# A two-layer mixture of experts that streams its weights from HBM: longer contiguous runs per partition, and fewer groups of 128 slots

## The chip, the cores and the metric

The kernel runs on one core of one Trainium2 chip. The metric is the device time of one execution in microseconds. The time before is 2375.89 us, the median of 3 runs (2375.29 to 2379.04).

## The reference, cut to what matters

The model is a block with two layers (attention, a mixer, then a mixture of experts) followed by a second block with two more layers and no experts. Only the mixture of experts is touched. It has 32 experts in 4 groups of 8; each token goes to 2 experts, and layer 0 has 512 tokens (`x` and `ctx`), layer 1 has 256.

```python
def run(args):                      # one block of token rows, one expert e
    xb, e = args
    return (jax.nn.silu(xb @ w1[e]) * (xb @ w3[e])) @ w2[e]
...
ys = lax.map(run, (xs, block_e)).reshape(-1, d_)
return jnp.zeros_like(h).at[slot_tok].add(ys * slot_gate[:, None])
```

`w1[e]` and `w3[e]` are 1024x512 float32, `w2[e]` is 512x1024 float32: 2 MB each, 6 MB an expert, 192 MB a layer, and all of it is read from HBM in each layer.

## The kernel before, in words

**Weights.** All large weights go through one stream of units of 1 MB (class `Stream`, tiles `wu`, 128 partitions x 2048 float32), issued in a fixed order by SP. A unit takes a free slot; SP waits at the DMA until the matmuls that last read the slot are done. In the experts' stage there are 10 slots in layer 0 and 11 in layer 1 that go round, and 3 more that are used once (`SLOTS`, `EXTRA`). An expert's weights are pushed by `push_ex` (L203): its number is in a register, and the unit holds `per` chunks of 128 rows of the matrix, 4 for `w1` and `w3`, 2 for `w2`. So an expert is 6 units: two for each matrix. Chunk `k` of the unit is row block `k`: partition `p` gets row `k*128 + p`, so that a partition's 8 KB come as 4 runs of 2 KB (`w1`, `w3`) or 2 runs of 4 KB (`w2`).

**Slots and groups.** The experts are ranked by their number of tokens (expert 0 always stands first, its units are loaded before the routing is known). `CAPS` (L43) gives rank by rank how many token slots an expert gets: 128 (or 256), 64 or 32. A group is 128 slots: one expert of 128 (kind `b`), two of 64 (`m`) or four of 32 (`s`). `make_plan` (L49) makes the groups; `ORDER` (L45) puts them into blocks. Before there are 16 groups in layer 0 (6 `b`, 7 `m`, 3 `s`) and 15 in layer 1 (7 `b`, 3 `m`, 5 `s`, the second expert having two `b` groups that share their weights). Where an expert has more tokens than its slots, a flag is set and a slow branch (`fallback`, L1347) runs over all experts.

**Work of a block** (`moe_main`, L1158). For each group stage A multiplies by `w1`, stage B by `w3`, stage C by `w2`; in a block all A come first, then all B, then all C. The four (two) experts of a group work in different columns of the PE array, so that a stage of a group has the same number of steps whatever its kind. A half stage needs the units of its half of *all* the group's experts, and hands them back at its end.

- *Gather* (`prep`, `step`, L1184): the block's token rows are brought into slots and transposed by matmuls of a one-hot matrix `G` with the tokens, kept as a pair of float32r tiles (`tok0h`, `tok0l`, in the second layer `tok1h`, `tok1l`). The tokens are the stationary operand, 128 columns `k*128 .. k*128+127` for chunk `k`; a chunk takes 2 matmuls per 128 tokens, 8 in layer 0 and 4 in layer 1. The next block's four steps stand in this block's C stages.
- *Transposes* (`tr`, L1311): before stage C the 128x512 product `sil` is transposed in four pieces.
- *Scatter* (`scatter`, L1222): a group's result goes back to the token rows by 16 matmuls in layer 0 (8 in layer 1), DVE multiplies by the gate row and POOL adds.

All matmuls are recorded at line 276, all transposes at line 314, the experts' DMAs at line 207.

Of the kernel before, what the change touches and what calls it, by code (L numbers as in the profile page):

```python
# [14 lines left out]
def _warn_once_fixed(msg, *args, **kwargs):  # L15
# [16 lines left out]
P = 128  # L32
# [7 lines left out]
NE = 32  # L40

NSTATIC = 1
CAPS = {4: [128] * 6 + [64] * 14 + [32] * 12,  # L43
        2: [128, 256] + [128] * 4 + [64] * 6 + [32] * 20}
ORDER = {4: ("bs", "bmmb", "smbm", "mbsm", "bm"),  # L45
         2: ("bs", "bbsm", "sbm", "sbm", "bsb")}


def make_plan(caps, order):  # L49


    lists = {"b": [], "m": [], "s": []}
    p = 0
    while p < len(caps):
        c = caps[p]
        if c >= P:
            lists["b"] += [(P, [p], b) for b in range(0, c, P)]
            p += 1
        else:
            n = P // c  # L60
            assert caps[p:p + n] == [c] * n
            lists["m" if c == 64 else "s"].append((c, list(range(p, p + n)), 0))
            p += n
    groups, blocks, stages = [], [], []
    for i, pat in enumerate(order):
        ids = list(range(len(groups), len(groups) + len(pat)))
        groups += [lists[ch].pop(0) for ch in pat]
        blocks.append(ids)
        seq = [(z, g) for z in "ABC" for g in ids]
        if i == 0:  # L70
            a, b = ids
            seq = [("A", a), ("B", a), ("A", b), ("B", b), ("C", a), ("C", b)]
        stages += [(i, z, g) for z, g in seq]
    assert not any(lists.values())
    return groups, blocks, stages


def constants():
# [16 lines left out]
    col = np.stack([31 - i + np.where(i < NSTATIC, 1 << 20, 0), i], 1).astype(f)  # L95
    cap4 = np.tile(np.array(CAPS[4], f), (P, 1))
    cap2 = np.tile(np.array(CAPS[2], f), (P, 1))
    out["cst_a"] = np.concatenate([ident, sel2, iota, rcol, w4, w8, col, cap4, cap2], 1)
# [40 lines left out]
class Stream:  # L139
# [62 lines left out]

    def push_ex(self, src, reg, k0, per, n):  # L203

        def fn(t):
            r = reg()
            self.last = self.nc.sync.dma_start(  # L207
                t[:, :per * n].rearrange("p (k f) -> p k f", k=per),
                src[ds(r, 1), k0 * P:(k0 + per) * P, :].rearrange("o (k p) f -> p (o k) f", p=P)).ins
        self.push(fn, 2)  # L210

    def get_kn(self, ks, n):
# [20 lines left out]
class Kern:  # L233
# [859 lines left out]
    def static_experts(self, l, NT):  # L1093
        if l:
            for c in range(0, D, 256):
                self.ws.push_kn(self.a["w_mk_2"][0][:, c:c + 256], KD, 256, 1, self.tc.issue_after(self.bc_last))
        groups, blocks, stages = self.plans[NT] = make_plan(CAPS[NT], ORDER[NT])
        n = 0
# [59 lines left out]
    def moe_main(self, l, NT, pl, tok, acc, G2, mp0, end_plan, load_numbers):  # L1158
# [4 lines left out]
        with ExitStack() as es:  # L1163
# [5 lines left out]
            def prep(b):  # L1169

                gb = [groups[g] for g in blocks[b]]
                n = len(gb) * P
                G = T([P, NT, 512], "G", 1, F32R)
                for i, (w, ps_, base) in enumerate(gb):
                    nj, p0 = len(ps_), ps_[0]
                    nc.vector.tensor_tensor(
                        G[:, :, i * P:(i + 1) * P].rearrange("p t (j w) -> p t j w", j=nj),
                        self.iota[:, base:base + w][:, None, None, :].to_broadcast([P, NT, nj, w]),
                        pl["pos"][:, :, p0:p0 + nj][:, :, :, None].to_broadcast([P, NT, nj, w]),
                        op=OP.is_equal)  # L1180
                Gf = G.bitcast(F32)
                xq = []

                def step(q):  # L1184
                    xt = T([P, 2, 512], "xT", 4)
                    for kk in range(2):
                        k = 2 * q + kk
                        ps = self.pt("t")
                        for t in range(NT):
                            for z, src in enumerate((tok.hi, tok.lo)):  # L1190
                                self.mm(ps[:, :n], src[:, t, k * P:(k + 1) * P], G[:, t, :n],
                                        t == 0 and z == 0, t == NT - 1 and z == 1)
                        self.ev(xt[:, kk, :n], ps[:, :n])
                    xq.append(xt)

                def gates():
                    pgate = self.pt("s")
                    for i, (w, ps_, base) in enumerate(gb):
                        for t in range(NT):
                            for j, p in enumerate(ps_):  # L1200
                                self.mm(pgate[w * j:w * (j + 1), i:i + 1],
                                        Gf[:, t, i * P + w * j:i * P + w * (j + 1)], pl["gs"][:, t, p:p + 1],
                                        t == 0, t == NT - 1)
                    gcol = T([P, 4], "gcol", 2)
                    nc.vector.tensor_copy(gcol[:, :len(gb)], pgate[:, :len(gb)])
                    return gcol
                return dict(xq=xq, step=step, gates=gates)

            def rows(g):
# [53 lines left out]
            for si, (b, z, g) in enumerate(stages):  # L1263
# [9 lines left out]
                if z in "AB":  # L1273
                    ps = self.pt("mm")
# [33 lines left out]
                h_ = sil.pop(g)  # L1308
                tp = self.pt("t")
                for f in range(4):  # L1310
                    self.tr(tp[:, f * P:(f + 1) * P], h_[:, f * P:(f + 1) * P])  # L1311
                hT = T([P, 4, P], "hT", 2)
                self.ev(hT.rearrange("p f s -> p (f s)"), tp)
                if not any(zz == "B" and bb == b for bb, zz, _ in stages[si:]) and b + 1 < len(blocks):
# [852 lines left out]
```

## Time and profile before

| | before |
|---|---|
| median of 3 runs | 2375.89 us |
| the profiled execution, its own time | 2375.62 us |
| its span, first to last instruction | 2374.0 us |
| experts of layer 0 on PE (A, B, C and all between) | 351 to 885 us of the span |
| experts of layer 1 on PE | 1120 to 1640 us of the span |
| moved by all DMAs | 598.60 MB, of it 384 units of the experts |
| PE busy | 2170.5 us (91%) |

A page of the profile shows one execution: busy time per engine, 40 slices of the span with the busy share of each engine, of the 16 DMA engines and their GB/s, the chain that ended last, and groups of like instructions. PE's busy time counts from an instruction's start to its end, with overlaps merged; matmuls follow each other faster than one of them lasts. A DMA share above 1 is possible, since packets of one DMA engine overlap.

### The profile page before, as it was taken

To read this page: it belongs to the slowest core of one execution; us is meant where nothing else is said; L and a number is where in the kernel's file an instruction comes from. 1 tells how busy PE (TensorE), PEld (TensorE's weight loads), DVE (VectorE), ACT (ScalarE), POOL (GpSimd) and SP (SyncE) were. 2 spreads that over 40 slices of the span, in tenths; PEclk is the share of its full clock that TensorE was granted. 3 is DMA by queue.
4 is the path that set the end of the run, shared out by engine and by line. 5 is a ranking of instruction groups with operands and counts; after the bars stand their busy time and mean duration, and the time that the engine had idled before them with its cause. 6 is when DMAs were issued, how large, how long until landed. Compare 5 with 4: busy or idle time off the path is not lost.

```text
span 2374.0 us, 32289 instructions
## 1 busy us (share of the span) xinstructions
PE 2170.5 (91%) x12723; PEld 1390.7 (59%) x12723; DVE 1004.6 (42%) x1963; ACT 702.8 (30%) x1267; POOL 399.9 (17%) x377
## 2 busy tenths in 40 slices
PE   7999979999998998998888887979999899999898
PEld 4565454443443436656333232325989799998797
DVE  3562562223131447624202212214566665565664
ACT  3344110010010114431110000002568464557653
POOL 0000221214051543012101202112100200100211
PEclk9998969999999998999889888989999899999999
DMA  9444569999999986464999999998444244443341
GB/s 311 137 132 167 200 215 345 387 351 334 400 391 385 401 319 220 156 216 170 342 337 384 384 400 387 400 386 293 152 143 138 91 164 142 143 155 113 107 142 46
DMA packets 330764, 598.60 MB, mean 252 GB/s; under 512 B 22218, under 2 KB 132330, under 8 KB 330604
## 3 DMA queue, kind: packets, MB, share of 16 engines
q1 hardware_dynamic: 322782, 579.22, 67.7%
q0 software_dynamic: 3728, 13.17, 1.6%
q10 hardware_dynamic: 4094, 4.05, 0.5%
q8 instruction: 103, 1.69, 0.3%
q14 instruction: 57, 0.47, 0.1%
HBM read 595.30 MB, written 1.10 MB: 251 GB/s over the span
## 4 chain that ended last, share of the span: by engine, by line
PE 36%; DMA 9%; issue 4%; DVE 2%; ACT 1%; SPq 1%; POOL 0%; DVEq 0%; ACTq 0%; POOLq 0%
PE psmm L276 31%; DMA wu<-in_w_dram 8%; PE pss L276 4%; PE pst L276 1%; PE pst L314 1%; SPq L207 1%; ACT wsplit L289 1%; DVE wsplit L293 1%; DVE yg L1231 0%; DMA c<-in_cst_dram 0%; DVE xd L1881 0%; DVE cvy L1863 0%; POOL mixA1l L293 0%; ACT dM L1922 0%; ACT yh L1339 0%
## 5 line engine op out<-in xcount | busy, mean ns | idle before, releaser
L276 PE MATMUL psmm<-wu,xT 128*32 128x512 f32 (+2 forms) x2080 | 480.4, 654 | 82.6 <-DMA wu<-in_w_dram 72.7
L276 PEld LDWEIGHTS psmm<-wu,xT 128*32 128x32 f32 (+2 forms) x2080 | 157.4, 144 | 370.0 <-issue 277.3
L1233 POOL TENSOR_TENSOR xs<-xs,yg 128x512 f32<-128x512 f32 x120 | 151.9, 1282 | 700.2 <-DVE yg L1231 699.6
L276 PE MATMUL psmm<-h2Th,wsplit 128*128 128x256 f32 x1344 | 258.1, 288 | 4.7 <-ACT zg L1850 3.7
L276 PE MATMUL psmm<-wu,hT 128*32 128x512 f32 (+2 forms) x1040 | 233.9, 633 | 17.0 <-DMA wu<-in_w_dram 16.9
L293 DVE TENSOR_TENSOR wsplit<-wu,wsplit 128x2048 fp32r<-128x2048 f32 x86 | 198.6, 2311 | 60.9 <-ACT wsplit L289 60.1
L276 PEld LDWEIGHTS psmm<-h2Th,wsplit 128*128 128x128 f32 x1344 | 212.9, 191 | 8.4 <-ACT zg L1850 3.9
L1231 DVE TENSOR_TENSOR yg<-pss,G 128x512 f32<-128x512 f32 x176 | 116.8, 687 | 231.5 <-PE pss L276 224.3
L289 ACT CAST wsplit<-wu 128x2048 fp32r<-128x2048 f32 x86 | 163.6, 1902 | 109.5 <-PE psmm L276 77.0
L276 PE MATMUL psmm<-h2Tl,wsplit 128*128 128x256 f32 x672 | 192.5, 287 | 0.0
L276 PEld LDWEIGHTS psmm<-wu,hT 128*32 128x32 f32 (+2 forms) x1040 | 76.4, 139 | 145.6 <-issue 123.5
L1289 DVE TENSOR_TENSOR sil<-sil,psmm 128x512 f32<-128x512 f32 x31 | 21.3, 687 | 317.6 <-PE psmm L276 317.6
L1339 ACT ACTIVATE yh<-psmm,gcol 128x512 fp32r<-128x512 f32 x62 | 41.8, 687 | 295.8 <-PE psmm L276 172.1
L276 PEld LDWEIGHTS psmm<-h2Tl,wsplit 128*128 128x128 f32 x672 | 128.5, 191 | 1.1 <-issue 0.7
L1287 ACT ACTIVATE sil<-psmm 128x512 f32<-128x512 f32 x31 | 18.5, 598 | 275.6 <-PE psmm L276 275.6
L276 PE MATMUL pss<-yh,S 128*128 128x512 f32 x176 | 86.1, 489 | 11.2 <-DVE yg L1231 9.9
L259 ACT COPY xT<-pst 128x512 f32<-128x512 f32 (+2 forms) x36 | 17.8, 497 | 247.7 <-PE psmm L276 146.1
L276 PE MATMUL psmm<-wu,mixT 128*128 128x512 f32 x192 | 90.4, 623 | 0.0
L1341 DVE SCALAR_TENSOR_TENSOR yl<-psmm,gcol,yh 128x512 fp32r<-128x512 f32 x62 | 45.9, 747 | 94.3 <-ACT yh L1339 93.2
L1233 POOL TENSOR_TENSOR cs<-cs,yg 128x512 f32<-128x512 f32 x62 | 77.9, 1278 | 46.1 <-DVE yg L1231 46.1
L519 DVE TENSOR_REDUCE mx<-psmm 128x1 f32<-128x256 f32 (+2 forms) x128 | 53.5, 452 | 50.0 <-PE psmm L276 49.8
L276 PEld LDWEIGHTS pss<-yh,S 128*128 128x128 f32 x176 | 33.1, 188 | 66.7 <-issue 33.5
(582 smaller groups left out, 3966.8 us busy)
## 6 DMA issues: line engine op xcount, KB each, us to landing
wu<-in_w_dram SPq DMA_DIRECT2D x384, 1024.0 KB
wu<-in_w_in_dram SPq DMA_DIRECT2D x62, 1024.0 KB
wu<-in_w_ada_dram SPq DMA_DIRECT2D x48, 1024.0 KB
wu<-in_w_out_dram SPq DMA_DIRECT2D x24, 1024.0 KB
wu<-in_w_mv_dram SPq DMA_DIRECT2D x8, 1024.0 KB
wu<-in_w_mq_dram SPq DMA_DIRECT2D x8, 1024.0 KB
wu<-in_w_mo_dram SPq DMA_DIRECT2D x8, 1024.0 KB
wu<-in_w_mk_dram POOLq DMA_DIRECT2D x4, 1024.0 KB, 12.1
```

The source lines that it names most:

```text
L207: self.last = self.nc.sync.dma_start(t[:, :per * n].rearrange("p (k f) -> p k f", k=per), src[ds(r, 1), k0 * P:(k0 + per) * P, :].rearrang ...
L276: return self.nc.tensor.matmul(out, lhsT, rhs, start=start, stop=stop).ins
L289: self.nc.scalar.copy(out.hi, src)
L293: e.tensor_tensor(out.lo, src, out.hi.bitcast(F32), op=OP.subtract)
L314: self.nc.tensor.transpose(out, in_, self.ident[0:n, 0:n])
L519: nc.vector.reduce_max(mx[:, i:i + 1], s[:, :nk], axis=AX.X)
L1231: nc.vector.tensor_tensor(y, ps, G2[:, who[t], c], op=OP.mult)
L1233: e.tensor_tensor(acc[t][:, c], acc[t][:, c], y, op=OP.add)
L1287: nc.scalar.activation(sil[g], ps, AF.Silu)
L1289: nc.vector.tensor_tensor(sil[g], sil[g], ps, op=OP.mult)
L1339: nc.scalar.activation(a_, yps[h], AF.Copy, scale=gc)
L1341: nc.vector.scalar_tensor_tensor(b_, yps[h], gc, a_.bitcast(F32), op0=OP.mult, op1=OP.subtract)
```

## The change

The run that a partition reads becomes 8 KB: in `push_ex` partition `p` takes the `per` consecutive rows `p*per .. p*per+per-1` instead of one row from each of `per` blocks. Chunk `k` of a unit then holds every 4th row (`w1`, `w3`) or every 2nd (`w2`) of its half, and the other operand is brought into the same order: the gather takes every 4th column of the tokens, and the transposes take every 2nd column of `sil`. At the same time `CAPS` moves ranks from 128 to 64 and from 64 to 32 slots: 14 groups in layer 0 (4 `b`, 6 `m`, 4 `s`) and 13 in layer 1 (5 `b`, 2 `m`, 6 `s`), in 4 blocks each instead of 5.

```diff
-CAPS = {4: [128] * 6 + [64] * 14 + [32] * 12,
-        2: [128, 256] + [128] * 4 + [64] * 6 + [32] * 20}
-ORDER = {4: ("bs", "bmmb", "smbm", "mbsm", "bm"),
-         2: ("bs", "bbsm", "sbm", "sbm", "bsb")}
+CAPS = {4: [128] * 4 + [64] * 12 + [32] * 16,
+        2: [128, 256] + [128] * 2 + [64] * 4 + [32] * 24}
+ORDER = {4: ("bs", "mmbs", "bmsm", "mbsm"),
+         2: ("bs", "bbsm", "sbms", "bss")}
...
-                src[ds(r, 1), k0 * P:(k0 + per) * P, :].rearrange("o (k p) f -> p (o k) f", p=P)).ins
+                src[ds(r, 1), k0 * P:(k0 + per) * P, :].rearrange("o (p k) f -> p (o k) f", p=P)).ins
...
                         ps = self.pt("t")
+                        o = k // 4 * 512 + k % 4
                         for t in range(NT):
                             for z, src in enumerate((tok.hi, tok.lo)):
-                                self.mm(ps[:, :n], src[:, t, k * P:(k + 1) * P], G[:, t, :n],
+                                self.mm(ps[:, :n], src[:, t, o:o + 4 * P - 3:4], G[:, t, :n],
...
                 for f in range(4):
-                    self.tr(tp[:, f * P:(f + 1) * P], h_[:, f * P:(f + 1) * P])
+                    o = f // 2 * 256 + f % 2
+                    self.tr(tp[:, f * P:(f + 1) * P], h_[:, o:o + 2 * P - 1:2])
```

The instructions on SP, in the first block of layer 0, where the units change from `w3` to `w2` (the shape is that of the destination, equal neighbouring dimensions joined). Before:

```order
L207 DMA wu_3448<-in_w_dram 128x4x512
L207 ISA
L207 DMA wu_3450<-in_w_dram 128x4x512
L207 ISA
L207 DMA wu_3452<-in_w_dram 128x2x1024
L207 ISA
L207 DMA wu_3470<-in_w_dram 128x2x1024
```

With the change:

```order
L208 DMA wu_3448<-in_w_dram 128x2048
L208 ISA
L208 DMA wu_3450<-in_w_dram 128x2048
L208 ISA
L208 DMA wu_3452<-in_w_dram 128x2048
L208 ISA
L208 DMA wu_3470<-in_w_dram 128x2048
```

The same units in the same order, but each is one run of 2048 elements per partition.

The instructions on PE at the start of the second block of layer 0 (`wu` are weight units, `xT` the gathered tokens; rows with 64 columns are a group of two experts). Before:

```order
L276 MATMUL pss_3781<-gs_2534,G_3539 128x1 x4
L276 MATMUL psmm_3808<-wu_3579,xT_3544 128x512 x2
L276 MATMUL psmm_3808<-wu_3579,xT_3603 128x512 x2
L276 MATMUL psmm_3808<-wu_3585,xT_3739 128x512 x2
L276 MATMUL psmm_3808<-wu_3585,xT_3760 128x512 x2
```

With the change:

```order
L277 MATMUL pss_3781<-gs_2534,G_3539 32x1 x16
L277 MATMUL psmm_3820<-wu_3585,xT_3544 64x512
L277 MATMUL psmm_3820<-wu_3579,xT_3544 64x512
L277 MATMUL psmm_3820<-wu_3585,xT_3544 64x512
L277 MATMUL psmm_3820<-wu_3579,xT_3544 64x512
L277 MATMUL psmm_3820<-wu_3585,xT_3603 64x512
```

The block begins with a group of two experts instead of a group of one: its first half stage reads two units where it read one. The block holds 54 units in 4 groups, where it held 36.

## Rows read from the trace of the kernel before

**Rows 1.** The page: span, the DMA rows of the 40 slices, and packets.

```profile
span 2374.0 us, 32289 instructions
...
DMA  9444569999999986464999999998444244443341
GB/s 311 137 132 167 200 215 345 387 351 334 400 391 385 401 319 220 156 216 170 342 337 384 384 400 387 400 386 293 152 143 138 91 164 142 143 155 113 107 142 46
DMA packets 330764, 598.60 MB, mean 252 GB/s; under 512 B 22218, under 2 KB 132330, under 8 KB 330604
```

**Rows 2.** Windows of both expert stages: length, engines' busy us (instructions), granted clock, DMA share, GB/s.

```profile
351.00:885.00 534.00, 506.87 (x2346) 223.29 (x2346) 152.31 (x236) 45.45 (x75) 158.04 (x140) 0.98 0.99 372
...
1120.00:1640.00 520.00, 433.88 (x2018) 171.67 (x2019) 95.83 (x163) 50.02 (x78) 72.49 (x71) 0.91 1.00 373
```

**Rows 3.** Windows within layer 0, the same columns.

```profile
362.00:430.00 68.00, 65.02 (x374) 32.82 (x372) 16.97 (x26) 6.17 (x10) 12.31 (x14) 0.97 1.01 382
430.00:545.00 115.00, 113.75 (x439) 50.84 (x437) 29.43 (x47) 9.97 (x17) 29.76 (x27) 1.00 0.95 350
545.00:850.00 305.00, 284.54 (x1401) 121.67 (x1399) 87.85 (x136) 24.19 (x41) 100.87 (x89) 0.98 1.03 390
850.00:885.00 35.00, 32.86 (x120) 13.11 (x116) 15.55 (x24) 4.53 (x6) 15.11 (x12) 1.00 0.92 325
```

**Rows 4.** Windows within layer 1, the same columns.

```profile
1120.00:1260.00 140.00, 114.68 (x538) 47.07 (x538) 21.00 (x41) 18.21 (x25) 11.71 (x14) 0.90 0.91 326
1260.00:1620.00 360.00, 302.19 (x1399) 117.57 (x1402) 69.42 (x114) 29.14 (x49) 55.47 (x52) 0.91 1.04 394
...
1350.00:1400.00 50.00, 37.04 (x172) 14.46 (x172) 4.99 (x8) 2.62 (x5) 0.00 (x0) 0.83 1.04 395
```

**Rows 5.** DMA view of 1340 to 1380 us: packets, and the queue of SP.

```profile
DMA packets 7777, 15.48 MB, mean 387 GB/s; under 512 B 234, under 2 KB 234, under 8 KB 7775
...
q1 hardware_dynamic: 7775, 15.45, 104.6%
```

**Rows 6.** DMA view of 1500 to 1520 us: packets, and the queue of SP.

```profile
DMA packets 2120, 8.18 MB, mean 409 GB/s; under 512 B 126, under 2 KB 126, under 8 KB 2119
...
q1 hardware_dynamic: 2119, 8.16, 102.3%
```

**Rows 7.** Waits of SP's DMA queue, layer 0 (351 to 885 us): us in total, times, longest.

```profile
SPq L207 <- PE psmm L276: 199.2, 55, 8.7
```

**Rows 8.** Waits of SP's DMA queue, layer 1 (1120 to 1640 us), the same columns.

```profile
SPq L207 <- PE psmm L276: 74.7, 33, 5.9
```

**Rows 9.** PE's groups in 351 to 885 us: busy us, mean ns of one, idle before, releaser.

```profile
L276 PE MATMUL psmm<-wu,xT 128*64 128x512 f32 (+2 forms) x1024 | 241.2, 615 | 18.6 <-DMA wu<-in_w_dram 11.9 <-PEq L1352 6.4 <-DVE yl L1341 0.3
L276 PE MATMUL psmm<-wu,hT 128*64 128x512 f32 (+2 forms) x512 | 117.7, 611 | 2.7 <-DMA wu<-in_w_dram 2.6
...
L314 PE MATMUL pst<-cst_a_sb,sil 128*128 128x128 f32 x64 | 10.5, 281 | 0.0
L276 PE MATMUL pss<-gs,G 128*64 128x1 f32 (+2 forms) x216 | 9.7, 201 | 0.3 <-DVE yg L1231 0.3
L276 PE MATMUL pss<-posS,sel 32*128 32x512 f32 x16 | 6.9, 469 | 1.3 <-DVE yg L1231 1.3
```

**Rows 10.** PE's first group in 1120 to 1640 us, the same columns.

```profile
L276 PE MATMUL psmm<-wu,xT 128*32 128x512 f32 (+2 forms) x1056 | 239.2, 692 | 64.0 <-DMA wu<-in_w_dram 60.8 <-PEq L1352 3.1
```

**Rows 11.** PE in order of time, gather and scatter matmuls: start, us, what.

```profile
396.67 0.39 PE L276 MATMUL pst<-G,tok0l 128*128 128x512 f32 x1
396.90 0.39 PE L276 MATMUL pst<-G,tok0h 128*128 128x512 f32 x1
...
398.30 0.40 PE L276 MATMUL pss<-yh,S 128*128 128x512 f32 x1
398.54 0.39 PE L276 MATMUL pss<-yl,S 128*128 128x512 f32 x1
```

**Rows 12.** Weight loads (PEld) in 351 to 885 us, columns as in rows 9.

```profile
L276 PEld LDWEIGHTS pst<-G,tok0h 128*128 128x128 f32 x128 | 24.1, 188 | 9.8 <-issue 4.1 <-ACT xT L259 1.8
```

**Rows 13.** PE in order of time, layer 0's last half stage and last scatter.

```profile
871.94 3.65 PE L276 MATMUL psmm<-wu,hT 128*64 128x512 f32 x16
...
875.52 0.50 PE L276 MATMUL pss<-yh,S 128*128 128x512 f32 x1
...
884.29 0.40 PE L276 MATMUL psmm<-yl,S 128*128 128x512 f32 x1
```

## The prediction, made before the changed kernel was run

> **What bounds the kernel now.** I read the page's slices first [rows 1]. The DMA engines are full (9 tenths) in two stretches, slices 7 to 14 and 20 to 27, at 334 to 401 GB/s; elsewhere they are mostly half idle. These stretches are the experts of layer 0 and layer 1; everything else in the kernel is untouched by the change, so only they are argued about.
>
> The windows [rows 2] show that the two stages have different limits. In layer 0 PE is busy for 506.9 of 534 us, and the DMA share is 0.99: both are near their end. In layer 1 PE is busy for 433.9 of 520 us at a DMA share of 1.00: the transfers set the pace. Who waits for whom agrees. In layer 0 SP waits 199.2 us in total for matmuls to hand slots back [rows 7], and PE waits for units only some 12 us in the large A/B group [rows 9]. In layer 1 SP waits 74.7 us [rows 8], and PE 60.8 us in that group [rows 10].
>
> Finer windows split layer 0 [rows 3]: from 430 to 545 us, in the block with two `b` groups and only 36 units, PE is the bound (113.8 of 115 us busy, transfers at 350 GB/s); from 545 to 850 us transfers are saturated (390 GB/s, share 1.03); and from 850 us on PE works off a backlog of 35 us with the last expert unit already on its way. In layer 1 the transfers are saturated from 1260 us to 1620 us (394 GB/s), with gaps before [rows 4].
>
> **The transfer rate.** Saturated stretches with only one kind of unit give a price per packet. From 1340 to 1380 us there were 7775 packets on SP's queue, 234 of them tiny; the 7541 others moved 15.45 MB, which is 2 KB each, the runs of `w1` and `w3` [rows 5]. On 16 engines that is one packet in 40 x 16 / 7541 = 84.9 ns, 387 GB/s. From 1500 to 1520 us the 1993 larger packets are of 4 KB, the runs of `w2`: one in 160.6 ns, 409 GB/s [rows 6]. So 2 KB more cost 75.7 ns, and each packet some 9 ns beyond its bytes. No packet of 8 KB is in this queue. **Bounds:** if a run of 8 KB goes as two packets of 4 KB, the rate is 409 GB/s; if the line holds, it takes 160.6 + 2 x 75.7 = 312 ns, which is 420 GB/s; without any cost beyond the bytes it would be 433 GB/s. I take 420, the straight line through both rows. The mix of today, two units at 387 for one at 409, makes 394, which is what the saturated window of layer 1 shows [rows 4].
>
> **The work on PE.** Stages A, B and C cost 241.2 + 117.7 us in layer 0 for 16 groups [rows 9], 22.4 us a group whatever its kind. Gather and scatter matmuls of 512 columns follow each other every 0.233 us [rows 11]: 16 for a group's scatter are 3.7 us, 64 for a block of four groups 14.9 us or 3.7 us a group. Transposes, gate columns and row selectors add (10.5 + 9.7 + 6.9) / 16 = 1.7 us. Together 31.5 us a group; 16 of them make 504 us, close to the 506.9 us of rows 2. Two groups fewer take **63 us** of PE work from layer 0, leaving 444. In layer 1 two of 15 groups are worth 2 x 433.9 / 15 = 58 us, but there PE is not the bound, and they only lengthen its waits: I cost them at nothing.
>
> **Layer 0.** From 362 to 850 us 68 x 382 + 115 x 350 + 305 x 390 us GB/s = 185.2 MB were moved [rows 3]; at 420 GB/s they need 441 us, 47 less. Then the tail: with transfers as the bound PE has little behind the last unit, about 2.5 us until it has landed (an estimate, one unit at 420 GB/s), a half stage of 3.65 us and the last scatter from 875.5 to 884.7 us [rows 13]: 15 us instead of 35, up to 19 less. So transfers alone would allow 66 us, PE alone 63. Both at once is only possible without any wait between them. With 507 us of work in 534 PE idles 5% today; in layer 1, with transfers well ahead of it as the bound, 17% [rows 2]. The new layer 0 stands between, with 444 us of work beside some 468 of transfers and tail; all three later blocks have the same kinds of groups and 54 units (56.6 MB, 135 us at 420 GB/s) beside about 4 x 31.5 = 126 us of PE work. I take 8% idle: 444 / 0.92 = 483 us, **51 us less**. Late next is then a unit for PE, not a slot for SP.
>
> **Layer 1.** From 1260 to 1620 us 360 x 394 / 420 = 338 us, 22 less. From 1120 to 1260 us the transfers pause for other reasons (326 GB/s at a granted clock of 0.90, share 0.91): their 45.6 MB take 116 us at 394 and 109 at 420 GB/s; I take half of this difference, 4 us. **26 us less.** PE is granted less than the full 2.4 GHz when it waits: 0.83 on average from 1350 to 1400 us, that is, part of the time at 1.2 GHz, after pauses for units. Yet the DMA share is 1.04 there [rows 4]: slower matmuls after a wait did not hold up the transfers. In layer 0 such pauses will be more frequent; this is part of the 8%.
>
> **The strided reads.** The gather's stationary operand now steps 4 float32, the transposes' 2. Weight loads of the gather take 188 ns with neighbouring columns [rows 12], behind matmuls that follow each other every 233 ns, so they are covered today. No row shows a strided load. Bounds: nothing, or the loads become the pace. Below 233 ns for a load they would stay covered; I take nothing. The 56 transposes of layer 0 are bounded by a doubling of 10.5 us for 64 [rows 9], some 9 us, and I take nothing for them as well. The Trainium skill's page "SBUF — State Buffer" (section "Door 1: The DMA port swizzle") speaks against the change here: it says that engine reads want at least two hits in a 16-byte line, and that every step to a new line is penalised, so that 4 float32 are as far as a stride is free; a step of 4 leaves one hit a line, a step of 2 leaves two. By that rule the gather pays and the transposes don't; this is the third rival below.
>
> **Sum.** 2375.6 us (the profiled execution's own time, its span and 1.6 us around it; the median of the runs is 2375.9) - 51 - 26 = 2298.6, say **2299 us**.
>
> **Rivals.**
>
> *Packets of 4 KB.* The run is one, but the DMA cuts it. For it: the largest packets of this queue are 4 KB; against it: these are also the longest runs there were. The Trainium skill's page "DMA: Bandwidth & Descriptors" (section "SWDGE vs HWDGE vs iDMA") fits this rival: it gives a packet as preferably at most 4096 B; no row here shows what happens above. At 409 GB/s layer 0's 185.2 MB need 453 us, 12 more than above, and layer 1 gains 360 - 347 = 13 and 2 instead of 26: 39 + 15 = 54 less, **2322 us**.
>
> *No waits between the two.* Layer 0 gives all of PE's 63 us, and layer 1 22 and the 9 us that the first stretch could give: **2282 us**. Against it: today's 27 us of idle PE in layer 0.
>
> *Gather slowed to twice its pace.* 0.466 instead of 0.233 us for each of 192 gather matmuls (three blocks) adds 45 us to layer 0's PE work, 489 us / 0.92 = 531: nearly all of its gain is gone. The first block's 64 stand ahead of the stage and may add up to 64 x 0.233 = 15 us, the 128 of layer 1 hide in idle time: 26 - 15 + 3 = 14 less, **2362 us**.
>
> *Gather slowed until it is slower than before.* The same mechanism at a larger price. PE becomes the bound of layer 0 again; with 5% idle the stage is longer than today by more than layer 1 gains once (444 + 256 x d) / 0.95 exceeds 534 + 26, so from d = 0.34 us, a matmul every 0.58 us. At four times the load, 0.75 us, d is 0.52 us: (444 + 133) / 0.95 = 607 us, +73 - 26 = 47 more, **2423 us**. Against it: it takes three times the 188 ns of rows 12.
>
> *The change doesn't do what it says.* Smaller groups may overflow into the slow branch. Counting the tokens per expert from the reference and its inputs, rank 4 of layer 0 has 57 for 64 slots and rank 16 has 28 for 32; in layer 1 ranks 4 and 8 have 28 and 19. None overflows; if one did, 32 experts x 24 products each with a load of its own would cost milliseconds. On SP the units do become single runs.
>
> **Chances.** The forecast 0.62 (its own range 2287 to 2312), packets of 4 KB 0.14, no waits 0.07, half of layer 0's gain lost to slots and cold matmuls (about 2325) 0.05, gather at twice its pace 0.07, slower gather 0.03, overflow 0.01, nothing at all 0.01. The range of 2276 to 2345 leaves out the last four. A measurement of this kernel can tell about 0.2% (5 us) from no change: faster 0.95, same 0.01, slower 0.04.
>
> **What would show it.** Right: the experts' 384 units make 384 x 128 = 49,152 packets instead of 256 x 512 + 128 x 256 = 163,840, so some 216,000 in all instead of 330,764 [rows 1], with 8 KB ones at about 312 ns, 420 GB/s in layer 1's saturated stretch; layer 0's stage near 483 us and layer 1's near 494; gather matmuls still 0.233 us apart; PE's wait for units in layer 0 longer than today's, SP's wait for matmuls shorter. Wrong: packets of 4 KB; gather matmuls farther apart, with PE busy in layer 0 above 480 us; the slow branch taken.

## The result and the profile after

| | before | changed |
|---|---|---|
| median of the runs | 2377.47 us (2375.29 to 2381.23, 4 runs) | 2310.97 us (2308.62 to 2314.05, 4 runs) |
| profiled execution, its span | 2375.6, 2374.0 | 2308.62, 2307.0 |

The ratio is 0.9719, with a 95% interval of 0.9701 to 0.9738: 66.5 us less, about 2.8%. The forecast was 2299 us, in a range of 2276 to 2345.

The page of the changed kernel, with the rows that answer to [rows 1]:

```profile
span 2307.0 us, 31821 instructions
...
DMA  9343658999999994547989999995444254443240
GB/s 320 129 146 133 214 205 344 420 420 405 381 408 388 421 375 131 205 169 275 371 352 393 402 420 421 422 413 180 143 133 146 81 176 147 145 148 110 92 158 35
DMA packets 216075, 598.58 MB, mean 259 GB/s; under 512 B 22218, under 2 KB 132330, under 8 KB 166764
```

216,075 packets instead of 330,764, of which 216,075 - 166,764 = 49,311 have 8 KB or more: the 49,152 of the experts' units and 159 others. The fullest slices now move some 420 GB/s.

To see where the 67 us of span went, read PE's rows in order of time for four marks: the first matmul of stage A and the end of the last scatter, in each layer.

| us | first A, layer 0 | its last scatter | layer 0 | first A, layer 1 | its last scatter | layer 1 | from there to the end |
|---|---|---|---|---|---|---|---|
| before | 351.3 | 884.7 | 533.4 | 1120.1 | 1644.4 | 524.3 | 729.6 |
| changed | 353.0 | 842.5 | 489.4 | 1076.0 | 1574.5 | 498.5 | 732.5 |

Layer 0 gives 44.0 us, layer 1 25.8 us. 1.7 us are lost ahead of layer 0, 1.9 won between the layers and 2.9 lost behind layer 1: 67.1 in all.

The windows of the changed kernel, columns as in [rows 2]: layer 0, four pieces of it, layer 1, and its saturated stretch:

```profile
353.00:843.00 490.00, 450.97 (x2240) 201.26 (x2240) 132.26 (x205) 39.35 (x63) 137.71 (x122) 0.98 0.97 398
...
353.00:400.00 47.00, 46.96 (x221) 23.32 (x222) 9.39 (x14) 3.63 (x6) 3.02 (x7) 0.97 0.84 328
400.00:450.00 50.00, 49.22 (x283) 24.65 (x281) 17.36 (x30) 4.39 (x8) 19.76 (x18) 0.97 1.01 421
...
550.00:600.00 50.00, 46.74 (x266) 18.28 (x268) 16.53 (x27) 3.06 (x5) 23.13 (x21) 0.90 0.89 355
...
700.00:750.00 50.00, 46.13 (x278) 18.14 (x274) 10.73 (x17) 3.77 (x6) 16.17 (x15) 1.00 0.93 383
...
1076.00:1575.00 499.00, 401.55 (x1995) 162.55 (x1995) 85.71 (x143) 44.15 (x67) 64.10 (x62) 0.88 0.95 386
1260.00:1550.00 290.00, 220.63 (x1160) 79.44 (x1156) 45.68 (x73) 17.73 (x29) 41.62 (x39) 0.85 1.00 417
```

Layer 0 still has no single limit: PE is busy 451 of 490 us (8.0% idle, before 5%), and the transfers run at 421 GB/s except in some pieces, where they pause for slots (in 550 to 600 us SP stands at one slot for 11.4 us, and no packet of 8 KB starts from 584.3 to 587.4 us). In layer 1 PE is busy only 80% of the time, and the transfers move 417 GB/s where [rows 4] had 394.

The DMA view of 1350 to 1400 us of the changed kernel, in which only experts' units move:

```profile
DMA packets 2892, 21.06 MB, mean 421 GB/s; under 512 B 322, under 2 KB 322, under 8 KB 322
...
q1 hardware_dynamic: 2890, 21.04, 101.2%
```

2892 - 322 = 2570 packets of 8 KB in 50 us on 16 engines: one in 311 ns. The straight line through the packets of 2 and 4 KB had given 312.

PE's groups in layer 0 of the changed kernel (353 to 843 us), columns as in [rows 9], and its waits, to be held against [rows 9] and [rows 7]:

```profile
L277 PE MATMUL psmm<-wu,xT 128*32 128x512 f32 (+2 forms) x1024 | 211.8, 625 | 23.1 <-DMA wu<-in_w_dram 18.9 <-PEq L1355 4.2
L277 PE MATMUL psmm<-wu,hT 128*32 128x512 f32 (+2 forms) x512 | 103.6, 605 | 1.0 <-DMA wu<-in_w_dram 1.0
...
L277 PE MATMUL pst<-G,tok0h 128*128 128x512 f32 x96 | 41.8, 435 | 0.0
L277 PE MATMUL pst<-G,tok0l 128*128 128x512 f32 x96 | 38.4, 400 | 0.0
```

```profile
SPq L208 <- PE psmm L277: 299.4, 78, 11.4
```

A, B and C cost 315.4 us for 14 groups, 22.5 each, as before. PE waits 19.9 us for units instead of 14.5. SP waits 299.4 us for slots instead of 199.2, although PE is less busy; the last section comes back to this.

The second half of the gather ahead of layer 0 (two groups, so 256 columns), like instructions taken together: count, shortest / median / longest in ns. Before, 340.9 to 345 us, and changed, 341 to 349 us:

```profile
L276 PEld LDWEIGHTS pst<-G,tok0h x16: 187/188/192, 341.0 to 344.4; 128*128 128x128 f32 x16
...
L276 PE MATMUL pst<-G,tok0l x16: 275/277/286, 341.2 to 344.6; 128*128 128x256 f32 x16
```

```profile
L277 PEld LDWEIGHTS pst<-G,tok0h x16: 308/330/331, 341.1 to 348.1; 128*128 128x128 f32 x16
...
L277 PE MATMUL pst<-G,tok0l x16: 392/438/439, 341.5 to 348.4; 128*128 128x256 f32 x16
```

The same 32 matmuls take 7.3 us from first to last start instead of 3.5: one in 0.235 us instead of 0.113. But the granted clock differs as well. Windows before (the first half of the gather, then this one), columns as in [rows 2]:

```profile
332.00:334.00 2.00, 2.00 (x11) 2.00 (x11) 0.32 (x2) 0.00 (x0) 0.00 (x0) 0.50 1.02 333
341.00:344.70 3.70, 3.70 (x38) 3.70 (x32) 1.01 (x3) 0.66 (x2) 0.00 (x0) 1.00 1.04 385
```

and changed:

```profile
341.00:345.90 4.90, 4.90 (x33) 4.89 (x27) 0.58 (x2) 0.65 (x2) 0.00 (x0) 0.50 1.01 426
346.00:348.50 2.50, 2.50 (x13) 2.50 (x12) 0.42 (x1) 0.00 (x0) 0.00 (x0) 1.00 1.02 423
```

At the lower clock (0.50, that is 1.2 GHz) neighbouring columns, too, have loads of 330 ns and one matmul in 0.213 us (before, 331.6 to 335.3 us); 4 apart it is one in 0.233. At the full clock (1.00, 2.4 GHz) it is 0.113 against 0.233 to 0.235: so in the changed kernel behind 346 us, and in the runs alone (below), whose first gather has the full clock from 342 us on. So with loads 4 apart the pace is the same at both clocks, that of matmuls of 512 columns at the full clock [rows 11]. Behind those the loads are nearly hidden; behind 256 columns they double the pace at the full clock and add a tenth at the lower one.

### The profile page after: what moved, and what is told of

Same layout as the page of the kernel before. It is cut to its first block, busy times and chain, and to the rows that moved or that the text cites. A ratio compares the mean times of both kernels' runs of the same rounds, so it can differ in the third digit from the quotient of the medians.

```text
span 2307.0 us, 31821 instructions
## 1 busy us (share of the span) xinstructions
PE 2078.5 (90%) x12559; PEld 1358.8 (59%) x12559; DVE 967.0 (42%) x1907; ACT 690.9 (30%) x1245; POOL 369.9 (16%) x349
## 2 busy tenths in 40 slices
DMA packets 216075, 598.58 MB, mean 259 GB/s; under 512 B 22218, under 2 KB 132330, under 8 KB 166764
## 4 chain that ended last, share of the span: by engine, by line
PE 57%; DMA 15%; issue 5%; DVE 5%; ACT 2%; SPq 1%; POOL 1%; DVEq 0%; ACTq 0%; POOLq 0%
PE psmm L277 44%; DMA wu<-in_w_dram 13%; PE pss L277 6%; PE pst L277 4%; PE pst L315 2%; DVE yg L1233 1%; DMA wu<-in_w_mv_dram 1%; ACT wsplit L290 1%; DVE wsplit L294 1%; SPq L208 1%; POOL xs L1235 1%; SPq L1129 1%; DMA wu<-in_w_in_dram 0%; DVE cvy L1866 0%; DVE hx L926 0%
## 5 line engine op out<-in xcount | busy, mean ns | idle before, releaser
L277 PE MATMUL psmm<-wu,xT 128*32 128x512 f32 (+2 forms) x2080 | 425.1, 661 | 84.9 <-DMA wu<-in_w_dram 77.9
L277 PEld LDWEIGHTS psmm<-wu,xT 128*32 128x32 f32 (+2 forms) x2080 | 135.3, 138 | 346.2 <-issue 269.8
L1235 POOL TENSOR_TENSOR xs<-xs,yg 128x512 f32<-128x512 f32 x104 | 131.4, 1281 | 663.1 <-DVE yg L1233 662.7
L277 PE MATMUL psmm<-wu,hT 128*32 128x512 f32 (+2 forms) x1040 | 209.9, 647 | 17.9 <-DMA wu<-in_w_dram 17.9
L1233 DVE TENSOR_TENSOR yg<-pss,G 128x512 f32<-128x512 f32 x152 | 101.7, 687 | 163.1 <-PE pss L277 148.7
L277 PEld LDWEIGHTS psmm<-wu,hT 128*32 128x32 f32 (+2 forms) x1040 | 64.6, 135 | 137.4 <-issue 113.9
L277 PE MATMUL pss<-yh,S 128*128 128x512 f32 x152 | 74.0, 487 | 16.9 <-DVE yg L1233 15.5
L1344 DVE SCALAR_TENSOR_TENSOR yl<-psmm,gcol,yh 128x512 fp32r<-128x512 f32 x54 | 39.8, 747 | 117.3 <-ACT yh L1342 116.4
L1235 POOL TENSOR_TENSOR cs<-cs,yg 128x512 f32<-128x512 f32 x54 | 68.0, 1278 | 34.1 <-DVE yg L1233 33.9
L277 PE MATMUL psmm<-wu,cT 128*32 128x512 f32 x384 | 59.8, 670 | 11.2 <-DMA wu<-in_w_ada_dram 8.8
```

The costliest lines, as they stand in the source:

```text
L277: return self.nc.tensor.matmul(out, lhsT, rhs, start=start, stop=stop).ins
L1233: nc.vector.tensor_tensor(y, ps, G2[:, who[t], c], op=OP.mult)
L1235: e.tensor_tensor(acc[t][:, c], acc[t][:, c], y, op=OP.add)
L1344: nc.vector.scalar_tensor_tensor(b_, yps[h], gc, a_.bitcast(F32), op0=OP.mult, op1=OP.subtract)
```

## The experiments

**Theory.** Layer 0 has two limits of nearly the same height, PE's work (the groups) and the transfers (the runs). Lowering one leaves the other, lowering both pays; what is left between them is look-ahead. Layer 1 has one limit, the transfers, so only the runs count. **Rivals.** The transfers set both layers; or the groups made all of layer 0's gain. For the 12 us by which the forecast was missed: strided reads against slots.

### One part at a time

*Runs alone:* the changed kernel with the old tables.

```diff
-CAPS = {4: [128] * 4 + [64] * 12 + [32] * 16,
-        2: [128, 256] + [128] * 2 + [64] * 4 + [32] * 24}
-ORDER = {4: ("bs", "mmbs", "bmsm", "mbsm"),
-         2: ("bs", "bbsm", "sbms", "bss")}
+CAPS = {4: [128] * 6 + [64] * 14 + [32] * 12,
+        2: [128, 256] + [128] * 4 + [64] * 6 + [32] * 20}
+ORDER = {4: ("bs", "bmmb", "smbm", "mbsm", "bm"),
+         2: ("bs", "bbsm", "sbm", "sbm", "bsb")}
```

> Runs of 8 KB with their strided operands, but the old tables: 16 and 15 groups. Theory (two limits): layer 0 keeps its 507 us of PE work (some 4 more for the strided gather) beside 441 us of transfers, so PE is its only limit; with 4 to 5% idle the stage is 525 to 532 us instead of 534, 2 to 9 less. Layer 1, which waits for transfers, keeps its gain of some 25. In all 27 to 38 less than before: 2338 to 2350. Rival (transfers set both layers, the groups matter little): nearly all of the 67 us, 2311 to 2318.

Measured: 2345.09 us, ratio 0.9867 (0.9851 to 0.9883).

*Groups alone:* the kernel before with the new tables, the same lines the other way round.

> 14 and 13 groups, but the old runs of 2 and 4 KB, so nothing strided. Theory (two limits): layer 0's 185 MB need 488 us at 390 to 394 GB/s whatever the groups, with a tail of 15 us behind the last unit instead of 35 and the old pauses: 505 to 520 us, 15 to 28 less; layer 1 is bound by transfers and gains 0 to 4. In all 15 to 30 less than before: 2347 to 2362. Rival (the groups made layer 0's gain): 40 or more less, 2337 or lower. If e1 and e2 together give clearly less than 67 us, the two edits need each other.

Measured: 2361.66 us, ratio 0.9947 (0.9933 to 0.9961).

| | layer 0 | layer 1 | median, less than before |
|---|---|---|---|
| runs alone | 531.9 (-1.5) | 495.9 (-28.4) | 31.4 |
| groups alone | 512.5 (-20.9) | 526.9 (+2.6) | 14.8 |
| both | 489.4 (-44.0) | 498.5 (-25.8) | 66.5 |

Windows of layer 0 and layer 1, runs alone:

```profile
354.00:886.00 532.00, 516.81 (x2346) 244.50 (x2346) 151.31 (x236) 45.46 (x75) 157.93 (x140) 0.98 0.92 370
1121.00:1617.00 496.00, 437.70 (x2038) 186.44 (x2039) 99.57 (x168) 51.34 (x79) 74.92 (x72) 0.93 0.96 391
```

and groups alone:

```profile
351.00:864.00 513.00, 458.50 (x2240) 189.70 (x2240) 132.03 (x205) 39.36 (x63) 137.42 (x122) 0.95 1.01 382
1096.00:1623.00 527.00, 403.87 (x1995) 154.60 (x1995) 85.15 (x142) 44.16 (x67) 64.03 (x62) 0.87 0.99 368
```

In layer 0, with runs alone PE is busy 517 of 532 us and the transfers idle (share 0.92); with groups alone the transfers are full (1.01) and PE idles 54 us. Each edit alone moves the limit to the other side: 1.5 and 20.9 us where both give 44.0. Both times lie where the theory had them, and both rivals fall. In layer 1 the runs give everything, as forecast; with fewer groups it is 2.6 us longer with old runs and with new ones, which is within what a single profile can tell (some 3 us, see below).

Runs alone also show what strided reads cost where PE is the limit. The last block of the old order has two groups. Its gather of 256 columns within layer 0, before:

```profile
L276 PE MATMUL pst<-G,tok0h 128*128 128x256 f32 x32 | 8.7, 308 | 0.5 <-ACT xT L259 0.5
L276 PE MATMUL pst<-G,tok0l 128*128 128x256 f32 x32 | 7.9, 281 | 0.0
```

and with runs alone:

```profile
L277 PE MATMUL pst<-G,tok0h 128*128 128x256 f32 x32 | 13.2, 412 | 0.5 <-ACT xT L260 0.5
L277 PE MATMUL pst<-G,tok0l 128*128 128x256 f32 x32 | 12.8, 398 | 0.0
```

26.0 us instead of 16.6 (sums of durations that overlap); by their starts the matmuls come one in 0.235 us instead of 0.117, some 7.5 us for 64, which is most of the 10 us by which PE's busy time grew (506.9 to 516.8). The new order has only blocks of four groups behind the first, 512 columns each. So the 1.5 us hold a price that the changed kernel doesn't pay: with PE as the limit, longer runs without it would have given layer 0 some 9 us (an estimate from these numbers). Those and the 20.9 of the groups still fall 14 short of 44.0.

### The length of the runs

```diff
-                t[:, :per * n].rearrange("p (k f) -> p k f", k=per),
-                src[ds(r, 1), k0 * P:(k0 + per) * P, :].rearrange("o (p k) f -> p (o k) f", p=P)).ins
+                t[:, :per * n].rearrange("p (k f) -> p k f", k=2),
+                src[ds(r, 1), k0 * P:(k0 + per) * P, :].rearrange(
+                    "o (j p i) f -> p (o j) (i f)" if per == 4 else "o (j p) f -> p (o j) f", p=P, j=2)).ins
...
-                        o = k // 4 * 512 + k % 4
+                        o = k // 2 * 256 + k % 2
...
-                                self.mm(ps[:, :n], src[:, t, o:o + 4 * P - 3:4], G[:, t, :n],
+                                self.mm(ps[:, :n], src[:, t, o:o + 2 * P - 1:2], G[:, t, :n],
...
-                    self.tr(tp[:, f * P:(f + 1) * P], h_[:, o:o + 2 * P - 1:2])
+                    self.tr(tp[:, f * P:(f + 1) * P], h_[:, f * P:(f + 1) * P])
```

> As the changed kernel, but every run is 4 KB: two neighbouring rows of w1 and w3 per partition, one of w2 as before; the gather then steps 2 float32, the transposes 1. Theory (straight line of packet times): 4 KB packets of 160.6 ns, 409 GB/s where saturated; layer 1 loses 290 x (420/409 - 1), some 8 us, layer 0 between 4 and 11: 2321 to 2330. Rival (beyond 4 KB the length no longer matters): 2309 to 2313. For the stride: the load of 128 columns 2 apart is 205 to 260 ns between 190 (neighbours) and 315 (4 apart) if each step costs; 190 if two hits in 16 bytes make it free.

Measured: 2321.93 us, ratio 0.9784 (0.9767 to 0.98). DMA view of 1400 to 1450 us:

```profile
DMA packets 5290, 20.42 MB, mean 408 GB/s; under 512 B 313, under 2 KB 313, under 8 KB 5286
...
q1 hardware_dynamic: 5286, 20.37, 102.2%
```

5290 - 313 = 4977 packets, one in 50 x 16 / 4977 = 160.7 ns, the price of [rows 6]. From 4 to 8 KB the straight line holds; layer 0 was 498.4 us and layer 1 509.6, 9 and 11 more than changed. The rival that beyond 4 KB the length no longer matters falls.

Weight loads in layer 0 of this kernel (2 apart in the gather, neighbours in the transposes):

```profile
L278 PEld LDWEIGHTS pst<-G,tok0h 128*128 128x128 f32 x96 | 18.8, 195 | 7.5 <-issue 4.1 <-DVE hT L267 0.3
...
L316 PEld LDWEIGHTS pst<-cst_a_sb,sil 128*128 128x128 f32 x56 | 6.2, 140 | 12.3 <-issue 8.1 <-DVE sil L1292 3.9
```

and of the changed kernel (4 apart in the gather, 2 apart in the transposes):

```profile
L277 PEld LDWEIGHTS pst<-G,tok0h 128*128 128x128 f32 x96 | 29.7, 309 | 4.8 <-issue 4.1 <-DVE hT L266 0.3
...
L315 PEld LDWEIGHTS pst<-cst_a_sb,sil 128*128 128x128 f32 x56 | 8.2, 205 | 11.6 <-issue 7.7 <-DVE sil L1291 3.9
```

For the gather: 188 ns for neighbours [rows 12], 195 for 2 apart, 309 for 4 apart. The granted clock in layer 0 was 0.98 before and in the changed kernel [rows 2]. The expectation had 205 to 260 for 2 apart if each step costs; it is nearly free.

### What the strided reads cost in time

*Nothing strided, the pairing of features with weight rows left out.* In the first version the test for the slow branch was also made one that is never true; in the second it is as in the changed kernel. Against the changed kernel:

```diff
-                        o = k // 4 * 512 + k % 4
...
-                                self.mm(ps[:, :n], src[:, t, o:o + 4 * P - 3:4], G[:, t, :n],
+                                self.mm(ps[:, :n], src[:, t, k * P:(k + 1) * P], G[:, t, :n],
...
-                    self.tr(tp[:, f * P:(f + 1) * P], h_[:, o:o + 2 * P - 1:2])
+                    self.tr(tp[:, f * P:(f + 1) * P], h_[:, f * P:(f + 1) * P])
...
-        with tc.If(fv > 0):
+        with tc.If(fv > 1):
```

> As the changed kernel with its 8 KB runs, but gather and transposes read neighbouring columns as before; it leaves out the pairing of features with weight rows, and the slow branch for overflow is never taken. So nothing is strided and nothing is paid elsewhere for it. Theory (the strided loads cost what the gather of the first blocks and the small excess of the others show): 3 to 6 us less than the changed kernel, 2305 to 2308. Rival (hidden entirely): within 1 us. Rival (all of the 12 us by which the changed kernel missed the forecast): 2299.

Measured: 2303.18 us, ratio 0.9695 (0.9676 to 0.9713). PE's first matmul of stage A in the changed kernel, in order of time, and in this one:

```profile
353.04 5.22 PE L277 MATMUL psmm<-wu,xT 128*128 128x512 f32 x8 [4.20 <-PEq L1355]
```

```profile
344.96 13.57 PE L277 MATMUL psmm<-wu,xT 128*128 128x512 f32 x31 [0.51 <-ACTq L1353]
```

The wait of PE's sequencer for the test had gone too, so this run mixed two things. The second version (without the change of the test, the last two lines of the diff):

> As c1_contiguous (8 KB runs, nothing strided, the pairing of features with weight rows left out), but with the test for the slow branch as in the changed kernel: in c1 PE no longer waited for that test, 4.2 us ahead of layer 0 in the changed kernel, so c1 mixed two things. Theory (part of c1's 7.8 us was the test): 2 to 5 us less than the changed kernel, 2306 to 2309. Rival (all of c1's gain was the strided reads): 2302 to 2304. Rival (all of it was the test): 2310 to 2312.

Measured: 2307.07 us, ratio 0.9696 (0.9674 to 0.9719). As this is close to the changed kernel's own interval, the changed kernel was run once more:

> The changed kernel once more, unaltered: a closer look at its time, since the experiments on the strided reads (c1, c2: ratio 0.970) and on the slots (v0: 0.971) lie within the interval of its first measurement, 0.9719 (0.9701 to 0.9738). Theory (strided reads and slots are worth some 4 us each): 0.971 to 0.973 again. Rival (the first measurement was high, and those differences are its error): 0.969 to 0.970.

Measured: 2311.5 us, ratio 0.9717 (0.9699 to 0.9734). Its layer 0 took 492.1 us in this profile and 489.4 in the first: a single profile's stage is good to some 3 us. The nine runs of the changed kernel have a mean of 2310.8 us (standard error 0.9), the five of the second version 2306.2 (1.8): the strided reads cost 4.6 us, with an uncertainty of 4. In the second version's layer 0 itself nothing is won (492.2 us). What can be seen of it is the first gather: from its first matmul to the first A it takes 22.2 to 23.0 us in all seven profiles with loads 4 apart, and 19.2 to 20.8 us in the six with neighbours or 2 apart that keep the test, so some 2.6 us less. In the second version's profile the gather began at 334.7 instead of 330.8 us, though, so that its first A was no earlier (353.9 us, changed 353.0). How much of the first version's further 4 us is the test, its runs do not tell.

*The same pairing kept, by storing the tokens with their features permuted.* First when they are split in two parts (`Pair` holds both):

```diff
-            self.split(tok[:, t, c], hx[:, c])
+            dst, src = tok[:, t, c], hx[:, c].rearrange("p (q m) -> p m q", m=4)
+            self.split(Pair(*(x.rearrange("p (m q) -> p m q", m=4) for x in (dst.hi, dst.lo))), src)
...
-                                self.mm(ps[:, :n], src[:, t, o:o + 4 * P - 3:4], G[:, t, :n],
+                                self.mm(ps[:, :n], src[:, t, k * P:(k + 1) * P], G[:, t, :n],
...
```

> As the changed kernel, but the tokens are stored with their features permuted when they are split in two parts, so that the gather reads 128 neighbouring columns again; the splitting reads hx 4 apart instead. Theory (the strided weight loads, 315 ns instead of 190, show only behind short matmuls): the gather of 256 columns ahead of layer 0 goes from 0.233 back to 0.117 us a matmul and those of 512 columns lose their small excess: 2 to 6 us less than the changed kernel, 2305 to 2309. Rival (loads hidden, nothing to win): within 1 us. Rival (the splitting pays more for its steps than the gather did): 2 to 8 us slower.

Measured: 2313.2 us, ratio 0.9734 (0.9719 to 0.9748). Rows in order of time of the splitting, changed kernel (two casts of 512 elements, one subtraction):

```profile
299.93 1.14 ACT L290 CAST tok0h<-hx 128x512 fp32r<-128x512 f32 x2 [0.83 <-DVE hx L926]
```

```profile
314.64 0.68 DVE L294 TENSOR_TENSOR tok0l<-hx,tok0h 128x512 fp32r<-128x512 f32 x1
```

and reading 4 apart:

```profile
305.87 2.17 ACT L290 CAST tok0h<-hx 128x512 fp32r<-128x512 f32 x2 [0.81 <-DVE hx L926]
```

```profile
321.64 1.06 DVE L294 TENSOR_TENSOR tok0l<-hx,tok0h 128x512 fp32r<-128x512 f32 x1
```

ACT needs 1.1 us instead of 0.6, DVE 1.06 instead of 0.68, on the way to the first gather, which began at 337.9 instead of 330.8 us (elsewhere it began up to 4 us late without such an edit). From there to the first A it took 19.9 us instead of 22.2. So the price moved to the splitting, and nothing is won. Then one step earlier, where `hx` is written 4 apart (and `B` read 4 apart):

```diff
-            e.tensor_tensor(hx[:, c], z[:, c], A[:, c], op=OP.mult)
-            e.tensor_tensor(hx[:, c], hx[:, c], B[:, c], op=OP.add)
+            e.tensor_tensor(hx[:, c].rearrange("p (m q) -> p q m", m=4), z[:, c].rearrange("p (q m) -> p q m", m=4),
+                            A[:, c].rearrange("p (q m) -> p q m", m=4), op=OP.mult)
+            e.tensor_tensor(hx[:, c].rearrange("p (m q) -> p m q", m=4), hx[:, c].rearrange("p (m q) -> p m q", m=4),
+                            B[:, c].rearrange("p (q m) -> p m q", m=4), op=OP.add)
...
```

> As the changed kernel, but the tokens' features are permuted where hx is first written (its product with A is written 4 apart; B is then read 4 apart), so that both splitting and gather read neighbouring columns. Theory (a write 4 apart costs nothing or little, a read 4 apart some 0.4 us more on DVE for 512 columns): the gather's gain of 2 to 6 us remains, less 1 to 3: 2306 to 2311. Rival (writes cost as reads do): as with the permuted splitting, 2312 to 2316.

Measured: 2313.46 us, ratio 0.9732 (0.9713 to 0.9751); the first gather began at 335.2 us. Nothing won either.

### Look-ahead and order in layer 0

*One slot less.*

```diff
-    SLOTS = (4, 4, {0: 2, 1: 3})
+    SLOTS = (4, 4, {0: 1, 1: 3})
```

> As the changed kernel, with one unit slot less for the experts of layer 0 (9 instead of 10 after the first block). Theory (layer 0's missing 6 to 8% are pauses of the transfers while all slots wait for PE, that is, too little look-ahead): a unit is 2.5 us of transfers, and layer 0 gets 6 to 11 us longer: 2317 to 2322, layer 1 unchanged. Rival (PE and transfers wait for other things, the look-ahead suffices): within 2 us of the changed kernel.

Measured: 2322.17 us, ratio 0.9788 (0.977 to 0.9805). Layer 0 took 499.6 us, 10.2 more, layer 1 499.9. Its window of layer 0, then that of the next kernel, with one slot more:

```profile
353.00:853.00 500.00, 449.33 (x2240) 200.68 (x2240) 131.28 (x205) 39.48 (x63) 137.04 (x122) 0.97 0.96 391
```

```profile
354.00:841.00 487.00, 448.56 (x2240) 201.08 (x2239) 134.89 (x209) 39.16 (x63) 137.72 (x122) 0.97 0.99 404
```

*One slot more,* with room from other buffers:

```diff
-    SLOTS = (4, 4, {0: 2, 1: 3})
+    SLOTS = (4, 4, {0: 3, 1: 3})
...
-                sel = T([32, nj, w], "sel", 2, F32R)
+                Sm = T([P, N], "S", 2, F32R)
+                sel = Sm[0:32, 0:P].rearrange("p (j w) -> p j w", j=nj)
...
-                y = T([P, 512], "yg", 3 if NT == 4 else 2)
+                y = T([P, 512], "yg", 2)
...
-            self.ws.extra(ex.enter_context(self.rpool(f"wx{l}")), self.EXTRA)
+            self.ws.extra(ex.enter_context(self.rpool(f"wx{l}")), 3 if l else 2)
...
-                hT = T([P, 4, P], "hT", 2)
+                hT = T([P, 4, P], "hT", 2 if l else 1)
```

> As the changed kernel, with one unit slot more for layer 0 after its first block (11 instead of 10; 13 in the first block as before). The room comes from one buffer less each for the scatter's eviction and for the transposed rows, and from building the row selectors in the buffer that the selection matrix takes later. Theory (look-ahead, the mirror of s1_slot_less): layer 0 gains 6 to 10 us if the missing buffers cost nothing, and 0 to 6 us of that are given back in the scatter, which waits for POOL's additions: 2301 to 2309. Rival (the missing buffers cost more than the slot gives): 2311 to 2325.

Measured: 2307.04 us, ratio 0.9714 (0.9691 to 0.9738). And with half of layer 0's scatter additions on DVE:

```diff
-                        e = nc.gpsimd if h or not end else nc.vector
+                        e = nc.gpsimd if h or (l and not end) else nc.vector
```

> As v0_slot_more, and in layer 0 every second addition of the scatter is done on DVE (0.7 us) instead of POOL (1.28 us), so that the evictions come free sooner in spite of the missing buffer. Theory: the slot's 6 to 10 us in full: 2300 to 2306. Rival (DVE, which also evicts, now delays the scatter): slower than v0_slot_more.

Measured: 2310.98 us, ratio 0.9723 (0.9704 to 0.9742). So 9, 10 and 11 slots: 391, 398 and 404 GB/s over the stage; PE idle 10.1, 8.0 and 7.9%; 499.6, 489.4 and 486.6 us. The step down costs 10 us, the step up gives at most 3, which a profile cannot tell from nothing, and no more in the runs (2307.04 and 2310.98 us). The mirror that was expected is not there: look-ahead seems to have been just enough. What a slot alone would give is not shown, since this one was paid for with other buffers.

*Another order:*

```diff
-ORDER = {4: ("bs", "mmbs", "bmsm", "mbsm"),
+ORDER = {4: ("bs", "mbsm", "mmsm", "bmbs"),
```

> As the changed kernel, with another order of layer 0's groups: blocks bs, mbsm, mmsm, bmbs instead of bs, mmbs, bmsm, mbsm, so that groups of four (s), which ask for transfers faster than they come, and groups of one (b), where transfers wait for slots, are spread otherwise, with the b groups at the end. Theory (pauses by slots, set by the order): 4 to 10 us less, 2301 to 2307. Rival (the sum of PE's work and of the transfers sets layer 0, not their order): within 2 us.

Measured: 2315.51 us, ratio 0.9749 (0.9733 to 0.9764). A miss: layer 0 took 498.2 us, 6 to 9 more than in the two profiles of the changed kernel. The order matters, as the theory had it, but a tally by hand of units and half stages gave the wrong sign. Why this order is worse stays open. No version beat the changed kernel by more than the measurement can tell.

## Why the prediction was right

The forecast was 10.0 us below the profiled execution (2298.6 and 2308.62). By its steps:

- **The transfer rate** was right to a part in a hundred: 311 ns for 8 KB, 420 GB/s. *Packets of 4 KB* is out: the packets have 8 KB, and the kernel with real 4 KB runs shows 408 GB/s and took 2321.93 us, where that rival had said 2322 (to the us by luck: its terms were 39 and 15 us, measured 35.0 and 14.7 in the layers and 4 outside them). The Trainium skill's page "DMA: Bandwidth & Descriptors" (section "SWDGE vs HWDGE vs iDMA") has, in its table on the descriptors that GpSimd writes, a packet as preferably at most 4096 B; on SP's queue here packets of 8192 B were faster (420 GB/s against 408), and the measurement decides.
- **Layer 0** was to give 51 us and gave 44. The share of idle time was as taken, 8.0%, which is luck to the tenth, as 8 was only chosen between today's 5 and layer 1's 17; the term that was too small is PE's work, 451 us instead of 444: 451 / 0.92 is 490 us. Of these 7 us the gather's 192 matmuls of 512 columns are some 3 (80.2 us, before 77.3), stages A to C 2, the transposes 1 (10.2 us for 56, before 10.5 for 64). This split is read from the groups' sums and not shown by a run: in the profile of the second version without strides PE is busy just as long, 452 of 492 us. Its reason, two limits that must both go down, is what the two single edits showed.
- **Layer 1** was to give 26 us and gave 25.8, at 417 GB/s instead of 420. Fewer groups won nothing there, as taken: alone they made it 2.6 us longer, while the runs alone gave 28.4, so that the match to 0.2 us is luck.
- **The strided reads**, taken as nothing, are the step that failed, by a small amount. Loads 4 apart are recorded with 309 ns in layer 0, above the prediction's bound of 233, and one follows the other in 0.233 to 0.235 us: nearly hidden behind 512 columns, double the pace behind 256 at the full clock. That adds some 2.6 us between the first gather and the first A, which came 1.7 us later, and without strides the kernel is 4.6 us faster, give or take 4. The rule of the Trainium skill's page "SBUF — State Buffer" (section "Door 1: The DMA port swizzle") was right about the gather: two hits in 16 bytes are free (195 ns against 188), one is not (309). It did not hold for the transposes, where 2 apart took 205 ns against 140. The rival *gather at twice its pace* had the right factor, but only for matmuls of 256 columns at the full clock, not for those of 512.
- **The waits.** PE's for units grew, as said. SP's for matmuls were to shrink and grew from 199.2 to 299.4 us: that sign was wrong. The single edits show where it came from: with groups alone they do shrink, to 145.1 us, and with runs alone they rise to 366.4.
- The rest of the 10 us: 1.9 won between the layers, 2.9 lost behind them, both unforeseen.

## What to carry to other kernels

Where two resources are both near their end, price an edit by what the other still needs: here 1.5 and 20.9 us alone (some 9 and 20.9 without the strided gather of the old order) became 44 together. Two packet sizes in a trace gave a line that held here at twice the larger one. Before a layout moves a stride to another engine, ask what each reader of it hides behind: the same load was nearly free behind 512 columns and doubled the time of 256. And before two windows of PE are compared, look at the granted clock of both.

## What the runs showed of the hardware

How long SP is held by the issue of one 1 MB unit goes with the number of its packets. All issues of 600 to 625 us, before (512 or 256 packets a unit) and changed (128): shortest / median / longest in ns.

```profile
L207 SPq DMA_DIRECT2D wu<-in_w_dram x12: 942/2188/2945, 597.7 to 621.8; - x12
```

```profile
L208 SPq DMA_DIRECT2D wu<-in_w_dram x10: 333/333/333, 600.5 to 624.4; - x10
```

These are stretches in which transfers set the pace. Over all of layer 0 the 179 issues took 372/1115/4691 ns before, 372/373/3205 with 4 KB runs and 332/333/1033 in the changed kernel; in layer 1 one of its issues took 3866 ns, too. So units of more packets are not always held for long, but often; with 128 packets nearly none is. What holds them is not shown.

This is why SP's total of waits rose while PE's demand fell. Added up, the 179 issues took 244.6 us before and 63.5 in the changed kernel: time that SP had spent inside issues it now spends at the next slot's semaphore. SP's waits for matmuls in layer 0, runs alone and groups alone (before 199.2 us, both 299.4):

```profile
SPq L208 <- PE psmm L277: 366.4, 86, 13.9
```

```profile
SPq L207 <- PE psmm L276: 145.1, 46, 10.9
```

The runs alone, at nearly the old work of PE, take issues down to 65.1 us and waits up by 167; the groups alone take waits down. Waits of the issuing engine are not to be compared across a change of its packets.
